# Prompt attention that keeps the weights of all query blocks by key block, and multiplies them with the values in products of up to 512 columns

## The chip, the cores and the metric

The kernel runs on one core of one Trainium2 chip. The metric is the device time of one execution in microseconds (us). An execution is also taken by the hardware profiler; its records are the trace from which all rows below come. The engines are called PE (TensorE, matrix products; PEld is its weight load), DVE (VectorE), ACT (ScalarE), POOL (GpSimd) and SP (SyncE, which here issues transfers). ACT and POOL issue transfers too.

## The reference

One inference step of a decoder with two layers and a width of 1024, for a prompt of 512 tokens and for 8 sequences of 4 new tokens each that have 2048 cached positions. Each layer normalises its input and runs three mixers on it: a stick-breaking attention (called sb here, 4 heads of 64), a forgetting attention (fox, 4 heads of 64) and a state-space scan. Gates merge the three, an output projection and a squared-ReLU MLP follow. Of the prompt the two attentions compute, cut to what matters:

```
def stick_breaking_core(q, k, v, q_pos, k_pos):
    z = einsum('bqhd,bkhd->bhqk', q, k) * (HEAD_DIM ** -0.5)
    mask = k_pos[None, :] < q_pos[:, None]
    log_keep = where(mask, log_sigmoid(-z), 0.0)
    later = cumsum(log_keep, axis=3, reverse=True) - log_keep
    w = where(mask, exp(log_sigmoid(z) + later), 0.0)
    return einsum('bhqk,bkhd->bqhd', w, v)

def forgetting_core(q, k, v, fq, fk, q_pos, k_pos):
    s = einsum('bqhd,bkhd->bhqk', q, k) * (HEAD_DIM ** -0.5) + (fq - fk)
    p = softmax(where(k_pos[None, :] <= q_pos[:, None], s, NEG_INF))
    return einsum('bhqk,bkhd->bqhd', p, v)
```

Both run over query blocks of 128 tokens. Query block b needs the key blocks 0 to b only.

## The kernel before

All tokens, 544 of them, stand in two halves of 272 columns (TH). Each weight matrix comes from memory in slabs `wr` and is split into a high part `wh` (by ACT) and a low part `wl` (by DVE); the activations are split in the same manner. A projection unit is then 24 products of 128 x 272: 16 with `wh` and 8 with `wl`, into the accumulators "g" or "z". Products of split operands pass PE once; products of plain fp32 operands, as all of those of the attention, pass it four times, and the trace keeps two records for each.

`prompt_attention` (L511) runs for sb and for fox in both layers. A pair c of heads stands in one tile of 128 rows, head e of the pair in rows 64e to 64e+63. For each c (2 of them) and each query block b (0 to 3) it multiplies queries with keys (L518: a row group of 64, n = 128(b+1) columns, one bank "z" for each head, rows `z<-half`), computes the weights on DVE, ACT and POOL (L521, tiles "tr"), turns each block of 128 x 128 of them on PE (L526, rows `t<-C,tr`), copies the turned blocks to the core's memory (ACT, L528) and multiplies them with the values (L533, 128 rows, 64 columns of PE for each head, rows `o<-tr,vn`): for key blocks k = 0 to b one product of 128 columns for either head. The result goes to y (ACT, L535). So there are 32 passes (c, b) in the program: 160 products with values and 64 with keys.

`weave` (L246) puts the generators of several parts of the program beside each other, so that PE has projection units between the steps of the attention. The scheduler of the tile framework, which knows what depends on what, then sets the final order on each engine; every engine runs its own list in order.

The cached keys and values are gathered by POOL's queue (L338, rows `kv<-in_cache_...`), 512 KB a piece. `Cached` (L565) issues gathers ahead, up to 7, into tiles of a pool `kvp` with 9 buffers; `take` hands them to the products. A buffer is free for the next gather when its last product has read it.

At the start ACT's queue gets the second half of x (L292, L293) right behind the parameters. While x comes, PE multiplies a tile of zeros with itself (L437). Then come the squares of x (ACT, L443), which a product with ones sums (`t<-ts,C`), and from these the first norm. `parameters` (L314) loads the page table and computes the indices `idx` of all gathers.

Of the kernel before, what the change touches and what calls it, by code (L numbers as in the profile page):

```python
# [174 lines left out]
def _trunk(ctx, tc, i, o, cc):  # L175
# [6 lines left out]
    hp = ctx.enter_context(tc.tile_pool(name="hp", bufs=11))  # L182
    kvp = ctx.enter_context(tc.tile_pool(name="kvp", bufs=9))
    tr = ctx.enter_context(tc.tile_pool(name="tr", bufs=4))
# [33 lines left out]
    def trt():  # L218
        return tr.tile([P, 512], F32, tag="tr", name="tr")

# [16 lines left out]
    def mm(out, w, x, **kw):  # L237
        n = float(np.prod(x.shape[1:]))
        pe["t"] += n * (1 if x.dtype == F32R else 4) * out.shape[0] / P / 2400
        nc.tensor.matmul(out, w, x, **kw)  # L240
# [50 lines left out]
    nc.scalar.dma_start(PC, i["params"])  # L291
    for u in range(2):  # L292
        nc.scalar.dma_start(x.tiles[u][:, :, TH:], i["x"][1, u])  # L293
    nc.gpsimd.dma_start(C[:, :P], i["consts"][:, :P])
# [137 lines left out]

    h = Feat(dtype=F32R), Feat(dtype=F32R)
    idle = trt()
    dve.memset(idle, 0.0)
    warm = bank("a")
    for _ in range(5):  # L437
        mm(warm, idle[:, :P], idle)
    for s in range(2):
        acc = bank("t")[:, :TH]  # L440
        for k in range(KD):
            q = tst()[:, :TH]
            act.activation(q, x.at(k, s * TH, (s + 1) * TH), AF.Square)  # L443
            mm(acc, ones, q, start=k == 0, stop=k == KD - 1)
        scaled(h, x, "norm1_g", 0, rsqrt(acc, 1.0 / D), s)
# [64 lines left out]

    def prompt_attention(r, y, weights):  # L511
        for c in range(2):
            for b in range(4):
                n = (b + 1) * P
                ws, wts, zs = [], [], [bank("z") for _ in range(2)]
                for e in (1, 0):
                    hr = slice(64 * e, 64 * e + 64)
                    mm(zs[e][:, :n], r["q"][hr, c, b * P:(b + 1) * P], r["kT"][hr, c, :n])  # L518
                for e in range(2):
                    ws.append(trt())  # L520
                    weights(ws[e], zs[e], n, 2 * c + e, b)  # L521
                yield 12.0
                for e in range(2):
                    pt = bank("t")
                    for k in range(b + 1):
                        turned(pt[:, k * P:(k + 1) * P], ws[e][:, k * P:(k + 1) * P], ident)  # L526
                    wts.append(trt())
                    act.copy(wts[e][:, :n], pt[:, :n])  # L528
                    yield 1.5
                acc = bank("o")[:, :P]  # L530
                for k in range(b + 1):
                    for e in range(2):
                        mm(acc[64 * e:64 * e + 64, :], r["vn"][:, k, (2 * c + e) * 64:(2 * c + e) * 64 + 64],  # L533
                           wts[e][:, k * P:(k + 1) * P], start=k == 0, stop=k == b)
                act.copy(y[:, c, b * P:(b + 1) * P], acc)  # L535
        r["prompt"] = True
# [120 lines left out]
    def sb_sample(l, r, y):  # L657
        k, v = "cache_sb_k", "cache_sb_v"
        jobs = key_jobs(l, k, 3)
        for c in (2, 1, 0):  # L660
            jobs += key_jobs(l, k, c) + value_jobs(l, v, c + 1)
        rows = Cached(jobs + value_jobs(l, v, 0), 7)
        rows.ahead()
# [37 lines left out]
    def fx_sample(l, r, y, sq):  # L701
# [3 lines left out]
        for c in (1, 2, 3):  # L705
            jobs += key_jobs(l, k, c) + value_jobs(l, v, c - 1)
        rows = Cached(jobs + value_jobs(l, v, 3), 7)
        rows.ahead()
# [520 lines left out]
    for l in range(DEPTH):  # L1229
# [8 lines left out]
        if l:  # L1238
            turn["tags"] = ("g",)
        run(some(gsb, 4))  # L1240
        if not l:
            parameters()
        run(some(gsb, 4))
        cs = conv_state(l)
# [121 lines left out]
```

## Time and profile before

| | us |
|---|---|
| Median of 3 runs (2012.42, 2017.52, 2018.73) | 2017.52 |
| Profiled execution | 2016.9 |
| Its span, from first to last instruction | 2014.9 |
| PE busy | 1946.5 (97%) |
| DVE busy | 1043.7 (52%) |
| ACT busy | 993.0 (49%) |
| POOL busy | 361.5 (18%) |
| Mean granted clock of PE | 0.988 |

The span is what the trace covers; the device time has 2.0 us more around it. A granted clock of 1 is 2.4 GHz, 0.5 is 1.2 GHz. A busy share is a mean over the span.

### The profile page before, as it was taken

How to read it: one execution, taken by the hardware profiler on the slowest of the kernel's cores; microseconds unless marked ns; L12 is line 12 of the kernel's file. 1: busy time of each engine (PE TensorE's matmuls, PEld its weight loads, DVE VectorE, ACT ScalarE, POOL GpSimd, SP SyncE). 2: the span in 40 equal slices, each digit the busy share in tenths (PEclk: the TensorE clock that was granted, in tenths of full speed). 3: DMA queues.
4: the chain of work that ended last, by engine and by line, in shares of the span. 5: the costliest groups of instructions: out<-in, count | busy, mean ns of one | idle time of the engine just before them, and what ended most of it. 6: DMA issues, size and time to landing. Idle time of an engine off the chain costs nothing.

```text
span 2014.9 us, 40892 instructions
## 1 busy us (share of the span) xinstructions
PE 1946.5 (97%) x17046; PEld 1803.4 (90%) x17046; DVE 1043.7 (52%) x2027; ACT 993.0 (49%) x2139; POOL 361.5 (18%) x430
## 2 busy tenths in 40 slices
PE   8999999999999999999999999999999999999997
PEld 7888777878899999999998887787788999999997
DVE  4475567545466444444555646684545554443445
ACT  5475557245565333333445645672566443333334
POOL 2233522243100000000023344213430000000000
PEclk9999999999999999999999999999999999999999
DMA  6665555487442233223356656537873412323222
GB/s 227 197 225 181 194 178 191 139 280 279 140 140 84 76 93 95 84 86 94 116 205 219 205 187 214 200 114 245 274 253 105 148 54 86 93 85 91 88 84 87
DMA packets 105932, 308.94 MB, mean 153 GB/s; under 512 B 17060, under 2 KB 33188, under 8 KB 105236
## 3 DMA queue, kind: packets, MB, share of 16 engines
q1 hardware_dynamic: 66740, 169.12, 27.2%
q0 software_dynamic: 37088, 134.86, 19.5%
q8 instruction: 133, 2.18, 0.4%
q10 hardware_dynamic: 1920, 2.37, 0.3%
q14 instruction: 51, 0.42, 0.1%
HBM read 291.74 MB, written 14.57 MB: 152 GB/s over the span
## 4 chain that ended last, share of the span: by engine, by line
PE 85%; DVE 4%; DMA 4%; ACT 4%; issue 2%; another core or an unknown queue 1%; POOL 1%; SPq 0%; DVEq 0%; ACTq 0%; POOLq 0%
PE g L240 51%; PE z L240 23%; PE s L240 4%; PE a L240 3%; PE o L240 2%; PE t L244 1%; DMA kv<-in_cache_sb_v_dram,idx 1%; DMA wr<-in_w_in_dram 1%; DMA kv<-rowsd 1%; DMA kv<-in_cache_fox_v_dram,idx 1%; DVE gt L423 1%; ACT wh L355 0%; DVE half L346 0%; DVE wl L356 0%
## 5 line engine op out<-in xcount | busy, mean ns | idle before, releaser
L240 PE MATMUL g<-half,wh 128*128 128x272 f32 x5504 | 813.4, 294 | 15.5 <-ACT gt L887 6.2
L240 PEld LDWEIGHTS g<-half,wh 128*128 128x128 f32 x5504 | 733.5, 191 | 56.0 <-issue 27.5
L355 ACT CAST wh<-wr 128x1024 fp32r<-128x1024 f32 x238 | 249.7, 1049 | 407.8 <-PE g L240 347.7
L240 PE MATMUL g<-half,wl 128*128 128x272 f32 x2752 | 427.8, 290 | 2.0 <-issue 1.9
L356 DVE TENSOR_TENSOR wl<-wr,wh 128x1024 fp32r<-128x1024 f32 x238 | 291.7, 1226 | 224.6 <-ACT wh L355 197.4
L240 PEld LDWEIGHTS g<-half,wl 128*128 128x128 f32 x2752 | 376.8, 190 | 6.5 <-issue 6.1
L240 PE MATMUL z<-half,wh 128*128 128x272 f32 x2112 | 309.4, 289 | 3.5 <-ACT half L345 3.5
L240 PEld LDWEIGHTS z<-half,wh 128*128 128x128 f32 x2112 | 282.9, 189 | 4.6 <-ACT half L345 4.0
L346 DVE TENSOR_TENSOR half<-gt,half 128x272 fp32r<-128x272 f32 x224 | 95.7, 438 | 154.0 <-ACT half L345 150.0
L240 PE MATMUL z<-half,wl 128*128 128x272 f32 x1056 | 165.6, 287 | 0.0
L338 POOL DMA_INDIRECT kv<-in_cache_sb_k_dram,idx x64 | 63.9, 998 | 565.5 <-PE g L240 493.1
L240 PEld LDWEIGHTS z<-half,wl 128*128 128x128 f32 x1056 | 145.4, 189 | 0.2
L1197 DVE TENSOR_TENSOR half<-half,g 128x272 f32<-128x272 f32 x128 | 56.0, 437 | 112.4 <-PE g L240 112.1
L345 ACT CAST half<-gt 128x272 fp32r<-128x272 f32 x224 | 93.0, 419 | 28.1 <-DVE gt L423 17.0
L240 PE MATMUL s<-kv,Q 128*32 128x128 f32 x2048 | 87.0, 283 | 10.7 <-issue 10.3
L1327 POOL TENSOR_TENSOR half<-half,gt 128x272 f32<-128x272 f32 x4 | 3.7, 946 | 495.2 <-ACT gt L401 495.2
L240 PEld LDWEIGHTS s<-kv,Q 128*32 128x32 f32 x2048 | 58.3, 112 | 33.5 <-issue 28.9
L1197 DVE TENSOR_TENSOR half<-half,z 128x272 f32<-128x272 f32 x128 | 55.6, 434 | 57.1 <-PE z L240 56.7
L338 POOL DMA_INDIRECT kv<-in_cache_sb_v_dram,idx x64 | 66.4, 1037 | 99.5 <-PE s L240 30.6
L240 PE MATMUL a<-kv,ts 128*32 128x256 f32 x1024 | 73.7, 396 | 8.8 <-DMA kv<-in_cache_sb_v_dram,idx 5.0
L338 POOL DMA_INDIRECT kv<-in_cache_fox_k_dram,idx x64 | 65.3, 1020 | 93.9 <-PE a L240 20.4
L338 POOL DMA_INDIRECT kv<-in_cache_fox_v_dram,idx x64 | 62.0, 968 | 101.0 <-PE s L240 51.5
(254 smaller groups left out, 2105.1 us busy)
## 6 DMA issues: line engine op xcount, KB each, us to landing
wr<-in_w_in_dram SPq DMA_DIRECT2D x98, 512.0 KB
wr<-in_w_up_dram SPq DMA_DIRECT2D x64, 512.0 KB
wr<-in_w_down_dram SPq DMA_DIRECT2D x64, 512.0 KB
wr<-in_w_o_dram SPq DMA_DIRECT2D x16, 512.0 KB
kv<-rowsd SPq DMA_DIRECT2D x12, 512.0 KB
kv<-in_state_ssm_dram SPq DMA_DIRECT2D x8, 512.0 KB
out_dram<-kv SPq DMA_DIRECT2D x8, 512.0 KB
wr<-in_w_ssm_out_dram SPq DMA_DIRECT2D x8, 512.0 KB
```

Of the source, the lines that this page charges most:

```text
L240: nc.tensor.matmul(out, w, x, **kw)
L244: nc.tensor.transpose(out, x, one)
L338: nc.gpsimd.indirect_dma_start(dst, None, rows, bass.IndirectOffsetOnAxis(ap=index, axis=0))
L345: act.copy(hi, src)
L346: dve.tensor_tensor(lo, src, hi.bitcast(F32), op=OP.subtract)
L355: act.copy(hi, raw)
L356: dve.tensor_tensor(lo, raw, hi.bitcast(F32), op=OP.subtract)
L423: dve.scalar_tensor_tensor(u, x.at(k, t0, t1), pc(gname, l, k), rb, op0=OP.mult, op1=OP.mult)
L1197: dve.tensor_tensor(x.at(m, t0, t1), x.at(m, t0, t1), b, op=OP.add)
L1327: pool.tensor_tensor(ot[:, k], ot[:, k], rb, op=OP.mult)
```

## The change

1. The turned weights of all four query blocks of a pair are kept in one tile "pt", ordered by key block: key block k holds the query blocks k to 3 side by side. When all four are there, one product for each head and key block, of (4 - k) x 128 columns, replaces those of 128 columns. One copy of 128 x 512 takes the result to y.
2. The two loads of the second half of x are issued by ACT behind the fourth square.
3. The warm-up is 16 products of 512 columns and 4 of 272 in single passes, instead of 5 of 512 in four passes.
4. To make room: the pool of the gathered pieces has 8 buffers instead of 9, the depth of `Cached` is 6 instead of 7, the pool "tr" has 3 buffers instead of 4, and the memory for descriptors of POOL's transfers is 8192 instead of 16384.
5. In layer 0 `parameters` runs one step of `qkv` earlier.

```
-    kvp = ctx.enter_context(tc.tile_pool(name="kvp", bufs=9))
+    kvp = ctx.enter_context(tc.tile_pool(name="kvp", bufs=8))
...
-        return tr.tile([P, 512], F32, tag="tr", name="tr")
+        return tr.tile([P, 512], F32, tag="tr", name="tr", bufs=3)
...
-    for u in range(2):
-        nc.scalar.dma_start(x.tiles[u][:, :, TH:], i["x"][1, u])
...
-    idle = trt()
-    dve.memset(idle, 0.0)
+    idle = tr.tile([P, 512], F32R, tag="tr", name="idle", bufs=3)
+    dve.memset(idle.bitcast(F32), 0.0)
     warm = bank("a")
-    for _ in range(5):
-        mm(warm, idle[:, :P], idle)
+    for n in 16 * (512,) + 4 * (TH,):
+        mm(warm[:, :n], idle[:, :P], idle[:, :n])
...
-            act.activation(q, x.at(k, s * TH, (s + 1) * TH), AF.Square)
+            square = act.activation(q, x.at(k, s * TH, (s + 1) * TH), AF.Square)
+            if s == 0 and k == 3:
+                with tc.issue_after(square.ins):
+                    for u in range(2):
+                        nc.scalar.dma_start(x.tiles[u][:, :, TH:], i["x"][1, u])
...
         for c in range(2):
+            wt = tr.tile([P, 2, 13 * P], F32, tag="pt", name="pt", bufs=1)
             for b in range(4):
...
                 for e in range(2):
-                    pt = bank("t")
+                    t = bank("t")
                     for k in range(b + 1):
-                        turned(pt[:, k * P:(k + 1) * P], ws[e][:, k * P:(k + 1) * P], ident)
-                    wts.append(trt())
-                    act.copy(wts[e][:, :n], pt[:, :n])
+                        turned(t[:, k * P:(k + 1) * P], ws[e][:, k * P:(k + 1) * P], ident)
+                    to = wt[:, e, b * P:b * P + (3 * b + 1) * P].rearrange("p (k t) -> p k t", t=P)[:, ::3]
+                    act.copy(to, t[:, :n].rearrange("p (k t) -> p k t", t=P))
                     yield 1.5
-                acc = bank("o")[:, :P]
-                for k in range(b + 1):
-                    for e in range(2):
-                        mm(acc[64 * e:64 * e + 64, :], r["vn"][:, k, (2 * c + e) * 64:(2 * c + e) * 64 + 64],
-                           wts[e][:, k * P:(k + 1) * P], start=k == 0, stop=k == b)
-                act.copy(y[:, c, b * P:(b + 1) * P], acc)
+            acc = bank("o")
+            for k in range(4):
+                for e in (1, 0):
+                    mm(acc[64 * e:64 * e + 64, k * P:], r["vn"][:, k, (2 * c + e) * 64:(2 * c + e) * 64 + 64],
+                       wt[:, e, 4 * k * P:(3 * k + 4) * P], start=k == 0, stop=k == 3)
+            act.copy(y[:, c, :NP], acc)
...
-        rows = Cached(jobs + value_jobs(l, v, 0), 7)
+        rows = Cached(jobs + value_jobs(l, v, 0), 6)
...
-        run(some(gsb, 4))
+        run(some(gsb, 3))
         if not l:
             parameters()
+        run(some(gsb, 1))
...
-    nc = _bacc.Bacc("TRN2", target_bir_lowering=False, num_devices=1)
+    nc = _bacc.Bacc("TRN2", target_bir_lowering=False, num_devices=1, dynamic_dma_scratch_size=8192)
```

The scheduler sets the order, so the change shows best in the lists of the engines. On PE, in layer 1 at the fox heads' pair c = 1, query block b = 3, this stood before (`s<-kv,Q` are products with cached keys, `t<-C,tr` turns of prompt weights, `o<-tr,vn` their products with values, `g` a projection unit):

```order
L240 MATMUL s<-kv,Q 32x128 x4
L244 MATMUL t<-C,tr 128x128 x4
L240 MATMUL o<-tr,vn 64x128
L240 MATMUL g<-half,wh 128x272 x16
L240 MATMUL g<-half,wl 128x272 x8
L240 MATMUL g<-half,wh 128x272 x4
L240 MATMUL g<-half,wl 128x272 x2
L240 MATMUL o<-tr,vn 64x128 x7
L244 MATMUL s<-C,ts 128x128 x4
```

The same place in the changed kernel:

```order
L240 MATMUL s<-kv,Q 32x128 x4
L244 MATMUL t<-C,tr 128x128 x4
L240 MATMUL g<-half,wh 128x272 x16
L240 MATMUL g<-half,wl 128x272 x8
L240 MATMUL g<-half,wh 128x272 x4
L240 MATMUL g<-half,wl 128x272 x2
L240 MATMUL o<-pt,vn 64x512 x2
L240 MATMUL o<-pt,vn 64x384 x2
L240 MATMUL o<-pt,vn 64x256 x2
L240 MATMUL o<-pt,vn 64x128 x2
L244 MATMUL s<-C,ts 128x128 x4
```

The single product with values ahead of the projection unit is gone, and the seven behind it, for this block, have become eight for all four blocks.

On PE, in layer 1 at the fox heads' pair c = 0, query block b = 3, its products with keys stood so before (`z<-half 128x512`, one for each head):

```order
L240 MATMUL o<-tr,vn 64x128
L240 MATMUL g<-half,wh 128x272 x8
L240 MATMUL g<-half,wl 128x272 x4
L240 MATMUL o<-tr,vn 64x128 x2
L240 MATMUL z<-half 128x512 x2
L244 MATMUL t<-C,tr 128x128 x3
L240 MATMUL g<-half,wh 128x272 x8
```

And so in the changed kernel:

```order
L240 MATMUL g<-half,wl 128x272 x8
L244 MATMUL t<-C,tr 128x128 x2
L240 MATMUL z<-half 128x512
L244 MATMUL t<-C,tr 128x128 x2
L240 MATMUL z<-half 128x512
L240 MATMUL g<-gt,C 128x272
L240 MATMUL g<-half,wh 128x272 x16
```

The two heads' products, which stood next to each other, have two turns of 128 x 128 between them. Over the whole program 11 of the 32 pairs of products with keys are parted before (2432 columns in all) and 18 after (5632 columns).

ACT's list at the start of the program, before (`ts<-half` are the squares of x, `wh<-wr` the high parts of the first weights):

```order
L291 DMA PC<-in_params_dram 128x140
L293 DMA half<-in_x_dram 128x4x272 x2
L443 ACTIVATE ts<-half 128x272 x4
L330 ACTIVATE mulc<-PC 64x1 x2
L355 CAST wh<-wr 128x1024
L443 ACTIVATE ts<-half 128x272 x2
L355 CAST wh<-wr 128x1024
L443 ACTIVATE ts<-half 128x272 x5
```

And in the changed kernel, whose lines have other numbers:

```order
L291 DMA PC<-in_params_dram 128x140
L441 ACTIVATE ts<-half 128x272 x4
L445 DMA half<-in_x_dram 128x4x272 x2
L328 ACTIVATE mulc<-PC 64x1 x2
L353 CAST wh<-wr 128x1024 x2
L441 ACTIVATE ts<-half 128x272 x7
L398 ACTIVATE gt<-t,epsb 128x272
```

The loads of the second half of x have moved behind four squares, and both casts stand ahead of the fifth square.

## Rows read from the trace of the kernel before

**Rows 1.** The profile's page: its first line, and busy time by engine.

```profile
span 2014.9 us, 40892 instructions
...
PE 1946.5 (97%) x17046; PEld 1803.4 (90%) x17046; DVE 1043.7 (52%) x2027; ACT 993.0 (49%) x2139; POOL 361.5 (18%) x430
```

**Rows 2.** Busy time by engine in two stretches, then granted clock, transfer share, GB/s.

```profile
250.00:400.00 150.00, 140.18 (x1231) 116.84 (x1232) 96.55 (x218) 80.59 (x208) 35.49 (x47) 0.96 0.51 166
550.00:1000.00 450.00, 449.75 (x3588) 448.92 (x3587) 213.89 (x372) 194.74 (x364) 0.00 (x0) 1.00 0.31 95
```

**Rows 3.** Groups of instructions by form, PE: busy us, mean ns, idle before.

```profile
L240 PE MATMUL o<-tr,vn 128*64 128x128 f32 x320 | 36.1, 286 | 0.0
```

**Rows 4.** The timeline of PE from 1482 us: start, duration, instruction, count of records.

```profile
1482.70 0.43 PE L240 MATMUL o<-tr,vn 128*64 128x128 f32 x2
1483.06 2.28 PE L240 MATMUL g<-half,wh 128*128 128x272 f32 x16
1485.17 1.15 PE L240 MATMUL g<-half,wl 128*128 128x272 f32 x8
1486.16 0.67 PE L240 MATMUL g<-half,wh 128*128 128x272 f32 x4
1486.66 0.41 PE L240 MATMUL g<-half,wl 128*128 128x272 f32 x2
1487.01 1.09 PE L240 MATMUL o<-tr,vn 128*64 128x128 f32 x14
1488.03 0.75 PE L244 MATMUL s<-C,ts 128*128 128x128 f32 x4
```

**Rows 5.** The timeline of PE from 305 us, brackets: idle before and releaser.

```profile
305.94 1.13 PE L240 MATMUL z<-half 64*128 64x512 f32 x4
307.00 0.87 PE L240 MATMUL o<-tr,vn 128*64 128x128 f32 x10
309.47 1.97 PE L240 MATMUL a<-kv,ts 128*32 128x256 f32 x32 [1.60 <-DMA kv<-in_cache_sb_v_dram,idx]
```

**Rows 6.** The timeline of PE from 284 us.

```profile
284.15 0.91 PE L240 MATMUL z<-half 64*128 64x384 f32 x2
284.99 0.52 PE L240 MATMUL g<-half,wh 128*128 128x272 f32 x2
```

**Rows 7.** Groups of instructions by form, ACT: the copies to y.

```profile
L535 ACT COPY half<-o 128x128 f32<-128x128 f32 x32 | 8.5, 265 | 5.1 <-PE o L240 4.5
```

**Rows 8.** The timeline of ACT from 5 us.

```profile
5.21 1.39 ACT L443 ACTIVATE ts<-half 128x272 f32<-128x272 f32 x4 [3.11 <-DMA half<-in_x_dram]
...
10.96 1.04 ACT L355 CAST wh<-wr 128x1024 fp32r<-128x1024 f32 x1 [4.18 <-DMA wr<-in_w_in_dram]
...
16.33 0.49 ACT L400 ACTIVATE gt<-t,epsb 128x272 f32<-128x272 f32 x1 [0.48 <-PE t L240]
```

**Rows 9.** The timeline of PE from 8 us.

```profile
8.15 2.00 PE L240 MATMUL t<-ts,C 128*128 128x272 f32 x8
12.38 3.91 PE L240 MATMUL t<-ts,C 128*128 128x272 f32 x8 [2.24 <-ACT ts L443]
```

**Rows 10.** Busy time by engine from 14 to 16 us, then granted clock.

```profile
14.00:16.00 2.00, 2.00 (x5) 1.18 (x4) 1.11 (x3) 1.45 (x5) 0.00 (x0) 0.50 0.79 225
```

**Rows 11.** Transfer queues from 2 to 9.3 us: packets, MB, time share.

```profile
q1 hardware_dynamic: 1255, 1.87, 74.9%
q10 hardware_dynamic: 667, 0.57, 24.8%
```

**Rows 12.** Waits of PE, whole span: what for, us, times, longest.

```profile
PE a L240 <- DMA kv<-in_cache_sb_v_dram,idx: 5.0, 4, 2.1
...
PE a L240 <- ACT gt L638: 2.2, 1, 2.2
```

**Rows 13.** Waits of POOL, whole span.

```profile
POOL kv L338 <- PE s L240: 139.7, 37, 20.1
```

**Rows 14.** Tile kv, 290 to 312 us: ns min/median/max, first and last start.

```profile
L338 POOL DMA_INDIRECT kv<-in_cache_sb_v_dram,idx x2: 939/1028/1117, 299.6 to 300.9; - x2
```

More of the change, by code (lines that the diff above doesn't have):

```diff
@@ L512, in prompt_attention @@
         for c in range(2):
+            wt = tr.tile([P, 2, 13 * P], F32, tag="pt", name="pt", bufs=1)
             for b in range(4):
                 n = (b + 1) * P
-                ws, wts, zs = [], [], [bank("z") for _ in range(2)]
+                ws, zs = [], [bank("z") for _ in range(2)]
                 for e in (1, 0):
@@ L706, in fx_sample @@
             jobs += key_jobs(l, k, c) + value_jobs(l, v, c - 1)
-        rows = Cached(jobs + value_jobs(l, v, 3), 7)
+        rows = Cached(jobs + value_jobs(l, v, 3), 6)
         rows.ahead()
```

## The prediction

> **What bounds the kernel now.** I read the busy times first. PE is busy for 97% of a span of 2014.9 us, no other engine for more than 52% [rows 1]. The windows then show where the rest lies: from 550 to 1000 us PE is busy for 449.75 of 450 us at full clock, while in a stretch with prompt attention, 250 to 400 us, it is busy for 140.2 of 150 at a granted clock of 0.96 [rows 2]. So in most places a product that PE no longer does, or does faster, comes off the end, as long as its next work is ready. The sum below is therefore one of PE's list, place by place, and what DVE, ACT and POOL save counts for nothing unless PE waits for them. It is made against the profiled execution's 2016.9 us, which is 0.03% below the median of the three runs, 2017.52.
>
> Two prices are needed. **A change of form:** PE's products come in forms (128 rows x 128 columns for projections, 64 x 128 for keys, 128 x 64 for prompt values, 128 x 32 for cached rows). Eight `wl` products stand from 1485.17 to 1486.16, 0.124 us each; the two at 1486.66 are followed by products with values at 1487.01, 0.35 us later instead of 0.25 [rows 4]. So a change of form costs about 0.10 us. The Trainium skill, page TensorEngine Tiling (Array Packing), section Key Properties, says that changing the mode of tiling drains TensorE; this trace agrees, with that 0.10 us.
>
> **A column:** two products with keys of 512 columns, one for each head, take from 305.94 to 307.00, 1.06 us [rows 5]; one alone of 384 columns takes from 284.15 to 284.99, 0.84 [rows 6]. That the pair takes only 0.22 more says that the heads of a pair run beside each other, and 0.22 us for 128 columns is 1.7 ns a column. With 1.67, 512 columns are 0.85 and 384 are 0.64, and both rows leave 0.20 for the form's entry and exit.
>
> **The products with values.** The 320 records before are busy for 36.1 us [rows 3]. In PE's timeline they stand in 60 stretches, because the scheduler puts the first product ahead of the other head's copy. By records: 35 stretches of 2, from start to next start 0.36 us (1482.70 to 1483.06) [rows 4]; 2 of 4 (0.37), 3 of 6 (0.58), 4 of 8 (0.59), 7 of 10 (0.80), 2 of 12 (0.81) and 7 of 14 (1.02, from 1487.01 to 1488.03) [rows 4]. These sum to 31.9 us; with 60 entries of 0.10 they hold PE for 37.9. (The 1.02 of fourteen records, which are seven products of 0.21 us, also says that heads run beside each other in this form.) After, a group has 512 + 384 + 256 + 128 = 1280 columns a head: 1280 x 1.67 ns = 2.13 us and 0.20 for entry and exit, 2.33. Eight groups are 18.7; the order shows one, layer 0's fox pair c = 0, cut into three pieces, which costs two entries and exits and some columns without a partner, 0.8. So 19.5 for 37.9: **-18.4 us.**
>
> **What the new order gives back.** The scheduler now parts 18 pairs of products with keys where it parted 11, with 5632 columns in place of 2432. Parted heads no longer run beside each other: 3200 x 1.67 ns = 5.3 us, and seven more entries and exits, 1.4: **+6.7.** Counted over PE's whole order there are 465 changes of form before and 403 after, 62 fewer. The values take 100 away (60 stretches to 10, two each), the parted pairs add 14, so 24 others came: turns and cached rows that stood side by side with value products now stand between projections. 24 x 0.10: **+2.4.** Sum of PE's stream: -9.3.
>
> **Copies.** ACT's 32 copies to y take 8.5 us [rows 7]; 8 of 512 columns replace them. PE never stood idle ahead of a value product (the 0.0 at the end) [rows 3], so what feeds them is early enough, and ACT, busy for 49% [rows 1], is not behind: 0.
>
> **The start.** The fifth square can't be made before a cast that stands ahead of it in ACT's list; that cast waits until 10.96 for the first weights [rows 8]. PE sums four squares until about 10, then waits 2.24 us until 12.38, and needs 3.91 us for the other four [rows 9], since its clock there is 0.50, the lower level [rows 10], after that wait. The norm follows at 16.33 [rows 8]. In the changed order both casts stand ahead of that square, 2.1 us instead of 1.04, but the weights come sooner: up to about 6.6 us (the end of the fourth square) ACT's queue carries nothing large, and in the trace it held 24.8% of the engines' time from 2 to 9.3 us beside SP's 74.9% [rows 11]. About 6 us of a quarter are 1.5 us; so the casts go from about 9.5 to 11.6 and the squares from 11.9 in a row. With PE at half clock (0.98 a product) the norm is at about 16.0, with full clock at 14.3. I take -0.7, near the half clock that the row has; bounds 0 and -2.0. The warm-up ends near 7.7 instead of 8.15 and hides: PE waits for squares behind it anyway; without that cover it would be 0.4 us.
>
> A rule speaks against this gain. The Trainium skill, page DMA: Bandwidth & Descriptors, section Queues, rings and completion order, says that a DMA engine takes turns between the queues that have work, a packet each. By it the deferred loads would, once issued, have half of the turns, and what the weights gained until 6.6 us would be lost again: the start's term is then 0 and the sum 2008.6. The row speaks of 3 to 1 in time for the whole window, but with larger transfers on SP's queue, and decides nothing between them.
>
> **Fewer buffers for gathers.** A gather can start when its buffer has been read: POOL waited 139.7 us in 37 waits for products with cached keys [rows 13], so one buffer fewer does start gathers later. What counts is PE's work between a buffer's last reader and the first reader of what comes into it. From the order with the trace's durations: its median over 96 takes falls from 19.1 to 17.8 us, those under 8 us go from 13 to 15, the least from 6.4 to 5.1. The last gather for the product at 309.47 was issued at 300.9 [rows 5, 14], so where transfers are dense 8.6 us lie between issue and use, and 8 us of cover are about where waits begin. Before, PE waits for gathered sb values in 4 takes, 5.0 us in all [rows 12]; the worst, 1.60 at 309.47 [rows 5] and its like in layer 1, get wider (7.4 to 11.6 us, 7.4 to 10.5), while others get tighter. I take +1.0; bounds -4 and +17 (0.18 us in each take). The earlier `parameters` and the smaller descriptor memory: 0: the first lets gathers begin one unit of 24 products sooner (3.1 us, from 1483.06 to 1486.16) [rows 4] and not later; POOL needs about 1 us for one gather's descriptors [rows 14] and waits for buffers, not for descriptors [rows 13]; without that cover it would be some 1 us in each late take.
>
> 2016.9 - 9.3 - 0.7 + 1.0 = 2007.9, so **2008.0 us**, own range 2002 to 2011.5. Its ends: below, the 24 new changes of form cost nothing (-2.4), the start gives -2.0 instead of -0.7 and the gathers -1.0 instead of +1.0, 5.7 in all; above, each of the 24 costs 0.2 (+2.4) and the gathers twice what I take (+1.0).
>
> **Rivals.** *Waits go too (13%).* The 1.60 and 2.1 us waits for sb values vanish with the wider places, and so does the 2.2 us wait for a small copy [rows 12], since in the new order 24 products of projections stand ahead of it. A wait of that size can bring a spell at half clock behind it: the 3.91 us behind the 2.24 us wait [rows 9, 10] are 2.0 more than at full clock; two such spells less are 4.0. 2016.9 - 9.3 - 0.7 - 3.7 - 2.2 - 4.0 = 1997.0. Against it: the waiting place may only move.
>
> *Given back as waits (24%).* Values of a pair now wait for the last of four query blocks, with a single "pt" tile: the copies of the next pair's first block must wait for the group. Where this leaves PE without work it waits about 1.9 us, like those that stand in the table of waits [rows 12], and pays a half-clock spell, 2.0. Two of these: 2006.9 + 7.8 = 2014.7, not to be told from no change.
>
> *Slower (8%): the gathers become the bound.* With depth 6, if the wait in each of 96 takes grows by over 0.17 us, the sum passes 2023. At 0.18 it is 2006.9 + 17 = 2024. For it: places of 5.1 us against the 8.6 us above. Against: only 15 takes lie under 8 us, and 13 did before with 5.0 us of waits. Wide values that don't run beside each other would give the same, 8 x 2.13 = 17 us; the 1.02 us above speaks against that.
>
> **Chances.** 0.3% (6 us) is about what a measurement of this kernel can tell from no change: faster is below 2011.5, slower above 2023.6. The forecast has 55%, all of its own range below 2011.5; with the 13% faster is 68%, same 24%, slower 8%. The range that leaves out the slower case and half of the best one is 1998 to 2015.
>
> **What would show it.** In the trace after: 8 groups `o<-pt,vn` of about 2.3 us each and near 19 us in sum; parted `z<-half` products of 512 columns taking 0.85 + 0.2 us each; squares five to eight in a row from about 11.9 us and the norm at 14.3 to 16.0; waits for `kv` under 8 us in sum. Wrong is the sum if value groups take over 3 us, if waits of PE for `kv` or for ACT's copies into "pt" exceed 8 us, or if the granted clock falls below 0.98.

## The result, and the profile after

The changed kernel takes 1994.94 us (median of 4 runs, 1992.4 to 1995.43) where the kernel before takes 2015.12 beside it (4 runs): a ratio of 0.989, 95% interval 0.9866 to 0.9913, so 18 to 27 us faster. The prediction was 2008.0 with a range of 1998 to 2015: the sign was right, the gain more than twice what was forecast. The profiled execution took 1994.71 us, 22.2 less than that of before.

The page of the changed kernel begins so:

```profile
span 1993.0 us, 40474 instructions
...
PE 1927.8 (97%) x16864; PEld 1791.6 (90%) x16864; DVE 1037.8 (52%) x2027; ACT 996.2 (50%) x2115; POOL 370.5 (19%) x430
```

PE is busy for 18.7 us less than in [rows 1] and still bounds the kernel. The two windows of [rows 2], after:

```profile
250.00:400.00 150.00, 141.25 (x1300) 118.04 (x1301) 93.25 (x215) 83.74 (x209) 41.38 (x49) 0.98 0.56 189
550.00:1000.00 450.00, 449.75 (x3587) 448.85 (x3586) 213.67 (x374) 191.11 (x356) 4.59 (x5) 1.00 0.31 96
```

From 250 to 400 us PE passes 1300 records where it passed 1231, though not quite the same work stands in the same window; from 550 to 1000 us nothing moved. The groups of PE by form that answer to [rows 3]:

```profile
L240 PE MATMUL o<-pt,vn 128*64 128x512 f32 x32 | 8.6, 618 | 0.0
L240 PE MATMUL o<-pt,vn 128*64 128x384 f32 x32 | 6.5, 486 | 0.0
L240 PE MATMUL o<-pt,vn 128*64 128x256 f32 x32 | 5.5, 381 | 0.0
L240 PE MATMUL o<-pt,vn 128*64 128x128 f32 x32 | 3.2, 276 | 0.0
```

The same place as in [rows 4], in PE's timeline after:

```profile
1463.09 0.41 PE L240 MATMUL g<-half,wl 128*128 128x272 f32 x2
1463.43 2.37 PE L240 MATMUL o<-pt,vn 128*64 128x512 f32 x16
1465.73 0.75 PE L244 MATMUL s<-C,ts 128*128 128x128 f32 x4
```

A group of all four key blocks holds PE for 2.30 us, from 1463.43 to 1465.73 (2.33 was the estimate with its entry). Two parted products with keys of 512 columns, in the timeline after (the pair of [rows 5] took 1.06 us together):

```profile
302.87 1.12 PE L240 MATMUL z<-half 64*128 64x512 f32 x2
303.92 1.14 PE L240 MATMUL g<-half,wl 128*128 128x272 f32 x7
...
305.24 1.12 PE L240 MATMUL z<-half 64*128 64x512 f32 x2
306.29 2.00 PE L240 MATMUL g<-half,wh 128*128 128x272 f32 x14
...
312.22 1.96 PE L240 MATMUL a<-kv,ts 128*32 128x256 f32 x32
```

Each takes 1.05 us alone, as priced. The last line is the products with cached values that waited 1.60 us in [rows 5]: there is no wait now (why is taken up below). The start, on ACT and then on PE, beside [rows 8, 9]:

```profile
8.60 1.04 ACT L353 CAST wh<-wr 128x1024 fp32r<-128x1024 f32 x1 [1.41 <-DMA wr<-in_w_in_dram]
9.90 1.04 ACT L353 CAST wh<-wr 128x1024 fp32r<-128x1024 f32 x1 [0.26 <-DMA wr<-in_w_in_dram]
10.86 1.39 ACT L441 ACTIVATE ts<-half 128x272 f32<-128x272 f32 x4
...
15.16 0.49 ACT L398 ACTIVATE gt<-t,epsb 128x272 f32<-128x272 f32 x1 [0.42 <-PE t L240]
```

```profile
7.31 1.99 PE L240 MATMUL t<-ts,C 128*128 128x272 f32 x8
11.34 3.79 PE L240 MATMUL t<-ts,C 128*128 128x272 f32 x8 [2.04 <-ACT ts L441]
```

The first weights come at 8.60 instead of 10.96, the squares stand in a row from 10.86, and PE, after a wait of 2.04 us, needs 3.79 us for products that take about 2 at full clock; the norm comes at 15.16 instead of 16.33. The waits of PE, to be read beside [rows 12]:

```profile
PE g L240 <- ACT gt L892: 10.2, 2, 6.3
PE s L240 <- issue: 8.8, 21, 1.0
PE z L244 <- DVE tr L497: 7.7, 4, 2.9
PE s L240 <- DMA kv<-in_cache_fox_k_dram,idx: 6.9, 5, 3.2
PE g L240 <- issue: 4.2, 8, 0.8
```

The figures are the sum in us, the number of waits and the longest. "issue" stands for waits of which the trace names no cause. Both waits of [rows 12] are gone, and others have grown: for the gate's copy on ACT (`gt`; 6.2 before), for fox keys (none before), and for a bank that the sb weights hold (1.7 before). And the place of the 2.2 us wait:

```profile
385.19 0.27 PE L244 MATMUL s<-C,zn 128*32 128x128 f32 x1
385.21 2.25 PE L240 MATMUL g<-half,wh 128*128 128x272 f32 x16
387.31 1.17 PE L240 MATMUL g<-half,wl 128*128 128x272 f32 x8
388.31 0.41 PE L240 MATMUL g<-half,wh 128*128 128x272 f32 x2
388.65 1.09 PE L240 MATMUL a<-vn,gt 32*32 32x512 f32 x8
389.67 2.48 PE L240 MATMUL s<-kv,Q 128*32 128x128 f32 x81
```

Between the turn of the new tokens' weights and their products stand 26 products of projections, and PE goes on without a wait.

### The profile page after: what moved, and what is told of

Same layout as the page of the kernel before. It is cut to its first block, busy times and chain, and to the rows that moved or that the text cites. A ratio compares the mean times of both kernels' runs of the same rounds, so it can differ in the third digit from the quotient of the medians.

```text
span 1993.0 us, 40474 instructions
## 1 busy us (share of the span) xinstructions
PE 1927.8 (97%) x16864; PEld 1791.6 (90%) x16864; DVE 1037.8 (52%) x2027; ACT 996.2 (50%) x2115; POOL 370.5 (19%) x430
## 4 chain that ended last, share of the span: by engine, by line
PE 87%; DVE 3%; DMA 3%; issue 2%; ACT 2%; POOL 1%; SPq 0%; another core or an unknown queue 0%; DVEq 0%; POOLq 0%; ACTq 0%
PE g L240 52%; PE z L240 24%; PE s L240 4%; PE a L240 3%; PE o L240 2%; PE t L244 1%; DMA kv<-in_cache_fox_k_dram,idx 1%; DMA raw<-rowsd 1%; DVE gt L421 1%; DMA wr<-in_w_in_dram 1%; DMA kv<-rowsd 0%; PE t L240 0%; PE s L244 0%; DVE half L344 0%; DMA wr<-in_w_down_dram 0%
## 5 line engine op out<-in xcount | busy, mean ns | idle before, releaser
L240 PE MATMUL g<-half,wh 128*128 128x272 f32 x5504 | 809.8, 293 | 16.5 <-ACT gt L892 10.2
L240 PE MATMUL s<-kv,Q 128*32 128x128 f32 x2048 | 80.1, 277 | 15.9 <-issue 8.8
L336 POOL DMA_INDIRECT kv<-in_cache_sb_v_dram,idx x64 | 72.5, 1133 | 103.3 <-PE a L240 27.6
L892 ACT COPY gt<-g 128x272 f32<-128x272 f32 x112 | 42.4, 380 | 76.8 <-PE g L240 62.4
```

Source lines behind the costliest of these rows:

```text
L336: nc.gpsimd.indirect_dma_start(dst, None, rows, bass.IndirectOffsetOnAxis(ap=index, axis=0))
L892: act.copy(c, unit(w, 0, h, s))
```

## The experiments

The same two programs gave two levels of time. Before took 2013 to 2015 us in the first comparison and in three of the series below, and 1973 to 1974 in the two others, so each run is compared with before in its own series. The record gives chip number 1 for the first series (2014 us) and for the second (1973 us), so the level does not seem to be a property of a chip. Each run has its ratio to before with the 95% interval.

| run | what is in it | median, before beside it (us) | ratio, interval |
|---|---|---|---|
| e1_start | start only | 2003.98, 2014.28 | 0.9951 (0.9936 to 0.9967) |
| e2_values | wide products and their room | 1991.65, 2014.28 | 0.9897 (0.9873 to 0.9921) |
| e3_heads | heads 1, 0; 128 columns | 2019.45, 2014.28 | 1.0027 (1.0007 to 1.0046) |
| e4_no_values | all but the wide products | 2023.65, 2014.28 | 1.0065 (1.0039 to 1.0092) |
| e5_room | buffers only | 1984.48, 1973.41 | 1.0053 (1.0035 to 1.0071) |
| e6_after | full change | 1968.02, 1973.41 | 0.9976 (0.9966 to 0.9985) |
| e7_q_dve | full change, zeros by DVE | 1968.65, 1973.41 | 0.9977 (0.9963 to 0.9991) |
| e8_warm | warm-up only | 1977.59, 1973.41 | 1.0021 (1.0012 to 1.003) |
| e9_before | before again | 2013.5, 2012.97 | 1.0009 (0.9993 to 1.0025) |
| e10_after | full change | 1992.32, 2012.97 | 0.9905 (0.9887 to 0.9923) |
| e11_values | as e2_values | 1994.16, 2012.97 | 0.9905 (0.9886 to 0.9924) |
| e12_start | as e1_start | 2003.79, 2012.97 | 0.9952 (0.9938 to 0.9966) |
| e13_wide01 | full change, heads 0, 1 | 2001.4, 2014.17 | 0.9938 (0.9916 to 0.9961) |
| e14_heads_start | heads 1, 0 and start | 2012.68, 2014.17 | 1.0003 (0.9981 to 1.0026) |
| e15_wn_dve | one copy by DVE | 2018.27, 2014.17 | 1.0028 (1.001 to 1.0046) |
| e16_heads_start_wn | e14 with that copy | 2014.31, 2014.17 | 1.0001 (0.9983 to 1.0019) |
| e17_heads_start_deep | e14, 10 buffers | 1976.32, 1973.69 | 1.001 (0.9998 to 1.0023) |
| e18_before_deep | before, 10 buffers | 1989.65, 1973.69 | 1.0076 (1.0061 to 1.0091) |

To see where time went, PE's span is split in one way for every trace: from each product's start to the next one's start, idle time of over 0.2 us put apart, and the rest counted at full clock, so that what half clock adds is a row of its own. The clock's record begins 3 to 6 us after PE's first product; the warm-up until then is in the row "all the rest". The row of keys holds 4.3 to 4.7 us of other small products `z<-half`. The traces are of single runs: that of e3_heads took 2010.03 us, 9 below its median, and that of e8_warm 1972.23, 5 below. In us:

```
                       before  e9_before   after  e10_after  e3_heads  e14_heads_start  e12_start   e8_warm  e6_after
products with values     32.4       32.1    19.2       19.2      24.0             24.0       32.5      32.3      19.2
products with keys       34.8       34.9    41.8       41.8      41.0             41.7       34.0      35.0      41.6
projections            1594.3     1594.3  1589.0     1589.5    1591.1           1589.0     1593.2    1591.0    1586.8
turns of weights         20.0       20.6    18.3       18.5      17.8             17.6       19.9      19.8      18.0
cached scores            79.3       78.0    75.9       75.6      79.4             78.5       75.7      68.1      66.2
idle over 0.2 us         56.3       57.6    54.0       50.3      56.1             61.0       52.0      37.9      41.3
added by half clock      21.0       14.7    20.0       16.9      24.6             25.4       17.1      10.4      16.2
all the rest            166.4      167.3   164.2      164.7     163.3            163.9     165.2     165.3     164.5
sum                    2004.5     1999.5  1982.4     1976.5    1997.3           2001.1     1989.6    1959.8    1953.8
```

**Parts alone (first series).** e1_start has the later loads and the warm-up; e2_values has the new `prompt_attention` and the smaller buffers; e3_heads changes one line of before; e4_no_values is the full change with the old `prompt_attention` and four "tr" buffers.

```
# e3_heads
                 for k in range(b + 1):
-                    for e in range(2):
+                    for e in (1, 0):
                         mm(acc[64 * e:64 * e + 64, :], ...
```

> Only the start is changed (loads of the second half of x behind the fourth square, warm-up in single passes); everything else is as before. Theory 1 (the start gives what the landmarks of the two traces show, the first weights in use at 18.4 instead of 19.6 us and the third slab at 40.2 instead of 43.2): 3 us faster, about 2012. Theory 2 (the start gives only what its own arithmetic shows, the rest of these 3 us came with the attention's order): 0.7 to 1.3 us faster, not to be told from no change.

> The wide products with values and the smaller buffers that make room for them (gathered pieces 8 and depth 6, three tr tiles, half the descriptor memory); start and place of the page table's load as before. Theory 1 (what PE's list saves, priced form by form, is all: 465 to 404 changes of form, value products 29.0 to 18.1 us, parted products with keys 29.4 to 36.9, in sum 5 us by list): 2008 to 2011. Theory 2 (the wide products also take away waits and half-clock spells of PE, some 9 us, which is what the prediction missed): 1996 to 2000. If 2, its trace has fewer waits or less half-clock work than before at the same places as the full change.

> The kernel before with one change: the products with values take the heads of a pair in the order 1, 0 instead of 0, 1. The products keep 128 columns and one copy for each query block. Theory 1 (the gain lies in the stretches, not in the columns: with this order the scheduler no longer puts a single product ahead, 422 changes of form instead of 465): by PE's list 5.9 us faster, 2009. Theory 2 (the wide columns are needed): within 2 us of before. Theory 3 (any new order of the attention shifts waits by as much as PE's list changes): anything from 2003 to 2017, and its waits, not its list, say why.

> Everything but the wide products: start, depth 6 and 8 buffers, half the descriptor memory, earlier page table; values as before, four tr tiles. Theory 1 (fewer buffers cost, +1 us, the start gives 3): 2013. Theory 2 (fewer buffers cost nothing, or shift gathers to better times): 2005 to 2012. A rival from the prediction (gathers become late): 2020 or more, with waits of PE for kv above 10 us.

The wide products with their smaller buffers give all of the gain (22.6 us), and the start alone gives 10 us, half of it: the parts do not add. Both are more than either of their theories allowed. The heads' order alone makes the products with values and keys 2 us shorter in sum, projections 3 and turns 2 to 3, and yet its median is 5 us above before, outside all three theories. Its trace, of a faster run, is no longer than those of before, so it does not show those 5 us. In its waits stands

```profile
PE a L240 <- DMA kv<-in_cache_sb_v_dram,idx: 10.1, 4, 3.6
```

where before had 5.0 [rows 12], and half clock added 24.6 us (21.0 and 14.7 before). Without the wide products the smaller buffers cost: e4_no_values is 20 us slower than e1_start, as the rival had it, and PE waited there for fox keys,

```profile
PE s L240 <- DMA kv<-in_cache_fox_k_dram,idx: 15.0, 8, 3.3
```

**Room, the full change again, one wait, the warm-up (second series).** e5_room has kvp 8, depth 6 and half the descriptor memory only; e8_warm the new warm-up only. e7_q_dve adds to the full change:

```
-        pool.memset(Q, 0.0)
+        dve.memset(Q, 0.0)
```

> The kernel before with the smaller buffers only: 8 for gathered pieces, depth 6, half the descriptor memory. By PE's list it costs 1.8 us (products with keys parted as after the full change). Theory 1 (fewer buffers make gathers late and PE's waits throw it to half clock): 2023 or more, 9 us or more over before, with waits for gathered rows above 10 us and over 25 us lost at half clock. Theory 2 (the loss of the run without the wide products came from its own order, not from the buffers): 2012 to 2018.

> The full change again, to compare it with the wide products alone on one chip. Theory 1 (the start adds its own 1.2 us to the wide products): 1 to 3 us faster than they were, 1989 to 1991. Theory 2 (start and wide products each move waits and half-clock spells, and these do not add): 1992 to 1997, so no faster than the wide products alone (0.9897 of before).

> The full change, with one more edit: the block of zeros of the cached queries is written by DVE instead of POOL, where it stands in line behind gathers that wait for buffers; ACT waited 2.06 us for it, and behind ACT PE waited 2.9 us for a bank, once in each layer. Theory 1 (that wait is real on PE's path): 5.8 us of waits gone, 1988 to 1990. Theory 2 (what PE waits for there is late in another way too, or the wait moves on): 1993 to 1996.

> The kernel before with the single-pass warm-up only, which ends ahead of the data that PE waits for, and otherwise moves a few products of the first unit. Theory 1 (what stands in PE's list and waits is all that counts): within 1 us of before. Theory 2 (a small shift at the start changes which later stretches run at half clock): more than 3 us either way, with waits and list as before and another sum of half-clock time.

Here the full change gives 5.4 us, not 20. Buffers alone cost 11 us, as theory 1 had it; the wait for fox keys is 9.0 us, that for sb values is gone. Half clock, which theory 1 put above 25 us, adds 15.5. In e7_q_dve the wait that was aimed at went and another grew; its waits and, above them, those of e6_after:

```profile
PE g L240 <- ACT gt L892: 9.8, 2, 6.1
PE z L244 <- DVE tr L497: 7.7, 4, 2.9
PE s L240 <- DMA kv<-in_cache_fox_k_dram,idx: 7.0, 7, 2.3
```

```profile
PE g L240 <- ACT gt L892: 14.0, 2, 7.9
PE s L240 <- DMA kv<-in_cache_fox_k_dram,idx: 7.9, 6, 4.0
...
PE z L244 <- DVE tr L497: 1.9, 2, 0.9
```

5.8 us off one and 4.2 onto the other: the time did not move. The warm-up alone is 4 us slower; a few products of the first unit change places with it, so the cause is not settled.

**Before, the full change and its parts side by side (third series).** No new edits.

> The kernel before, unchanged, for a profile and a time on the same chip as the next three. The first two series ran at 2014 and 1973 us for the same program, and PE's waits of which the trace names no cause (issue) were 18.3 us in the first trace and none in those of the second series. Theory 1 (these waits are the chip's or the session's, not the kernel's): if the time is near 1973, no such waits and 8 to 16 us less than before in waits of under 0.2 us; if near 2014, some 18 us of them again. Theory 2 (they are the program's): some 18 us whatever the time.

> The full change on the same chip. Theory 1 (the gain has a part that PE's list carries, some 10 us, and a part that hangs on how starved PE is of instructions, 5 to 10 us): 4 to 10 us faster than before where the waits without a cause are near 0, 18 to 22 where they are near 18. Theory 2 (half-clock time by chance decides): anything between, with the sum lost at half clock as the difference.

> The wide products with their room alone on the same chip. Theory 1 (as the full change without the start): within 3 us of it, 4 to 10 us faster than before on a chip with few waits without a cause. Theory 2 (wide products gave all of the 22.6 us because of something that stays): 20 us or more faster on any chip.

> The start's edits alone on the same chip. Theory 1 (the start gives what its landmarks show, and what came behind them in the first series were other waits and half-clock time): 2 to 5 us faster. Theory 2 (the 10 us of the first series are its own): 8 to 12 us faster on any chip.

At 2013 us the waits with no cause in the trace are back. e9_before first, then e10_after:

```profile
PE s L240 <- issue: 10.0, 24, 1.0
PE g L240 <- issue: 6.1, 13, 1.1
```

```profile
PE s L240 <- issue: 9.2, 23, 1.2
...
PE g L240 <- issue: 4.6, 9, 0.8
```

In the second series e6_after, the same program, has no such wait. Over all traces these waits sum to 11.5 to 18.9 us in each of the 14 at the slower level and to 0.2 us or less in each of the 6 at the faster one. So they belong to the series and not to the program. The full change gains 20.6 us and the start 9.2 here, as in the first comparison and the first series: theory 1 of e12_start (2 to 5) fell. The wide products alone gain 18.8, so the start adds nothing to them that can be told apart.

**Width or order, and the wait in layer 0 (fourth series).** e13_wide01 writes `for e in range(2)` over the wide products; e14_heads_start joins e3_heads and e1_start; e15_wn_dve and e16_heads_start_wn change in before and in e14_heads_start:

```
-        act.copy(wn, b[:NS, :P])
+        dve.tensor_copy(wn, b[:NS, :P])
```

> The full change with one difference: the wide products with values take the heads in the order 0, 1, as the kernel before did. By PE's list there are 426 changes of form instead of 403, and heads of a pair do not run beside each other where the first is put ahead. Theory 1 (what shortens PE's list is that nothing stands between the heads of a pair, not the width): about 10 us slower than the full change, within 10 us of before. Theory 2 (the width does it): within 3 us of the full change.

> The kernel before with the order of heads 1, 0 and the start's edits: products of 128 columns, all buffers as before. Theory 1 (list and waits both count: the heads' order took 10 us off the list but left the waits and half-clock time of layer 0, which the start's edits took away): 15 to 20 us faster where before takes 2014, as fast as the full change. Theory 2 (the wide products are needed): no faster than the start alone, 0.995 of before.

> The kernel before with one copy (the turned weights of the new tokens, for which PE waits 2.2 us once in layer 0, ahead of two half-clock stretches) made by DVE instead of ACT. Its list of PE is 4.6 us longer. Theory 1 (that wait starts the half-clock stretches of layer 0, and both go): 3 to 8 us faster in spite of the list. Theory 2 (the half-clock stretches come from elsewhere): 0 to 5 us slower.

> The heads' order, the start's edits and the copy by DVE together, as a candidate against the full change. Theory 1 (the wait for that copy is gone already with the start's edits): as the second run within 3 us. Theory 2 (it was still there in part): 3 to 6 us faster than the second run.

With the heads in the order 0, 1 the wide products lose about a third of the gain (0.9938 for 0.9905 in the third series; the intervals just meet), which is between the two theories. With the order 1, 0 and 128 columns nothing is gained at all, though its values, keys, projections and turns are in sum within 4 us of the full change's. Idle time is 61.0 us and half clock adds 25.4 (52.0 and 17.1 in e12_start), and the wait for sb values is

```profile
PE a L240 <- DMA kv<-in_cache_sb_v_dram,idx: 10.1, 3, 5.0
```

The copy by DVE did not take its wait away: PE waited 3.5 us in two places for it, and the kernel was slower. Theory 1 fell in e14_heads_start and e15_wn_dve; in e16_heads_start_wn it held, since that run is within 2 us of e14_heads_start.

**One more buffer (fifth series).** kvp 10, depth 8, half the descriptor memory, in e14_heads_start and in before.

> The heads' order and the start's edits with 128-column products, now with one buffer more for gathered pieces (10, depth 8; half the descriptor memory makes room). Without the buffer PE waited 10.1 us for sb values. Theory 1 (what the shorter list saves is lost at gathers that come late): the waits for sb values fall below 4 us and it is 5 to 10 us faster than before. Theory 2 (these waits have another cause than a missing buffer): they stay at 8 us or more and the time at that of before.

> The kernel before with the same extra buffer, as the control. PE's list is 4 us longer by its order. Theory 1 (one buffer fewer cost 0.53%, so one more gives something): waits for gathered rows go, and it is 0 to 5 us faster. Theory 2 (at 9 buffers the gathers wait for PE's order, not for room): 2 to 6 us slower, by its longer list.

The waits for sb values did not fall. e17_heads_start_deep and e18_before_deep:

```profile
PE a L240 <- DMA kv<-in_cache_sb_v_dram,idx: 11.0, 2, 6.4
```

```profile
PE a L240 <- DMA kv<-in_cache_sb_v_dram,idx: 7.1, 2, 3.7
```

All eleven traces with 9 or 10 buffers have this wait (3.6 to 12.8 us), and of the nine with 8 buffers only one (1.0); these have waits for fox keys of 3.2 to 15.0 instead, which the others have at 4.0 or less. So the number of buffers, with the depth that goes with it, decides which of the gathers comes late, not whether one does.

## Why the prediction was right in sign and wrong in size

Against the mean of the two traces of before, the mean of the two after is 22.6 us shorter (2002.0 to 1979.4); the sum had said 9.0. The split says where: values -13.0, keys +7.0, projections -5.0, turns -1.9, cached scores -2.9, idle -4.8, half clock +0.6, the rest -2.4.

**Products with values (-18.4 with their entries): right.** From their first start to what follows they lost 13.0 us, where 31.9 less 18.5 (ten stretches without their entries) had been 13.4; the rest of the term was entries, which the split books with other products.

**Parted products with keys (+6.7): right.** The products of 64 rows alone grew by 6.6 us; 5.3 for the columns and 0.7 for seven exits had been 6.0.

**Other changes of form (+2.4): wrong.** What is booked with projections and turns, the entries saved and those that were to come back, should have been about -1.9 (62 fewer changes less the 50 exits of value stretches, plus 7 of keys: 19 at 0.10). It was -6.9; in the second series, between e8_warm and e6_after, -6.0. Even if the 24 changes that came back cost nothing, only -4.3 is explained (43 at 0.10); what saved the rest is open. This is some 5 us of the miss.

**The start (-0.7): the norm's mechanism right, the size low.** Squares in a row from 10.86 (predicted 11.9), the norm 1.2 us sooner and at half clock in this trace; in e1_start PE waited 1.22 instead of 2.04 us there, stayed at full clock, and the norm came at 13.67:

```profile
11.53 2.10 PE L240 MATMUL t<-ts,C 128*128 128x272 f32 x8 [1.22 <-ACT ts L441]
```

That is 2.7 us sooner, somewhat beyond the lower bound of -2.0 (a norm at 14.3). But the edit alone gave 10.3 and 9.2 us (e1_start, e12_start), far outside the bounds of 0 and -2.0: the term followed the norm only and took all that comes behind it as fixed. The weights came 2.4 us sooner, where 1.5 was the estimate. The transfer queues from 2 to 9.3 us, after, to be read beside [rows 11]:

```profile
q1 hardware_dynamic: 1470, 2.28, 91.7%
q10 hardware_dynamic: 265, 0.13, 8.2%
```

ACT's queue moved 0.13 MB, which is what its constants and parameters come to (64 and 70 KB). The loads of x, issued at 5.50 and 6.16 us, had moved nothing by then: their first packet starts at 9.43, 3.9 us after the first issue (before, 3.8 us: issued at 1.75, first packet at 5.53). Once they move, both queues have work; from 10 to 11 us, after:

```profile
q10 hardware_dynamic: 269, 0.29, 93.6%
q1 hardware_dynamic: 264, 0.03, 21.4%
```

269 packets of one queue and 264 of the other agree with what the Trainium skill, page DMA: Bandwidth & Descriptors, section Queues, rings and completion order, says of turns between queues. The rival that drew on it failed on the time: the second weights were in use at 9.90, when the loads of x had only just begun to move.

**Fewer buffers (+1.0): too small for the edit alone, and not to be read off in the full change.** Alone, the buffers cost 11.1 us (e5_room), inside the bounds of -4 and +17. With the wide products the waits for gathered rows are 6.9 and 4.4 us in sum (after, e10_after), where they were 5.2 and 4.9 before.

**Waits without a cause and cached scores, put at nothing: this step failed, beside the changes of form.** The sum had one term for waits, +1.0 for late gathers. The table of PE's waits of before, from which [rows 12] are cut, begins with a line that it left out, and has a second two lines below:

```profile
PE s L240 <- issue: 10.3, 27, 1.0
...
PE g L240 <- issue: 6.0, 12, 0.8
```

No term stood for these, and no reason was given. PE's whole table of waits, in us (it counts waits from 0.15 us on):

```
                    before  e9_before   after  e10_after  e12_start   e8_warm  e6_after
no cause (issue)      18.3       18.6    13.7       14.5       18.5       0.2       0.0
with a named cause    40.1       40.7    42.3       38.4       35.6      40.0      43.0
```

Waits with a named cause are the same before and after (40.4 in the mean of two): what the prediction held against its rival, that the waiting place may only move, came true. Waits without a cause fell by 4.4 us, and the cached scores by 2.9 (by 1.9 in the second series), for which the sum had no term either. With the 5 us of changes of form that is 12 of the 13.6 us by which the sum missed; what is left lies in the row "all the rest". Why the full change has fewer waits without a cause is open. At the faster level, which has none, it gives 5.4 us, less than the 9.0 of the sum: there, between e8_warm and e6_after, values, keys, projections and turns lose 12.5 us, but named waits take back 3.0 and half clock 5.8.

**The rival at 1997.0 came within 2 us of the result by luck.** Its two waits, for sb values and for the small copy, did go in the full change. But both also went in e5_room, with the old products, which is 11 us slower than before: the wait for sb values is gone or 1.0 in every trace with 8 buffers, so the smaller pool is enough to remove it, without wider places. The wait for the small copy is absent from 16 of the 20 traces, among them e3_heads, e4_no_values, e14_heads_start and e18_before_deep, none of them faster than before. Other waits grew in their place (fox keys 6.9, the bank 7.7, the gate's copy 10.2), and of its 4.0 us at half clock nothing came (17.9 to 18.5). None of the signs that the prediction named as wrong appeared either: groups of 2.30 us, waits for `kv` of 6.9, for the copies into "pt" of 1.7, a clock of 0.987. They looked only for a result that is too slow.

Why the parts do not add is open too. The start alone and the wide products alone both lose the wait for the small copy, but so do slower kernels, so that wait is not what they share. In the split both shorten the cached scores (78.7 to 75.7 and 76.5 with the start, to 75.0 and 74.2 with the wide products), and the full change does so only once (75.9 and 75.6); beyond these 2 to 4 us nothing is shown.

**Open.** Why a list as short gives 20 us with wide products and nothing with 128 columns in the heads' order is only half answered: with 128 columns the gain was taken back as idle time and half clock, with sb values waiting 10 us. More buffers did not help; the heads' order with 8 buffers was not tried, nor the earlier page table by itself. The two levels of time, too, have no cause here. No run beat the full change: the wide products alone were as fast where both ran in one series.

## What to carry to other kernels

On an engine that is busy for 97%, sum the list of products place by place, but give waits a term of their own with both signs, those without a named cause too: here values, keys, projections and turns explained 13 of 23 us. A wait that goes is no proof that its going brought the gain: look whether it went in the slower runs too. An edit that shortens the list ahead of a late transfer may only lengthen the wait for it, so test a saving with and without the reordering that comes with it. Gains of two edits measured alone (20 and 10 us here) need not add, and a gain found on one level of time (20 us) can be a quarter of that on another.

## What the runs showed of the hardware

The same program ran at 2013 to 2015 us in some series and at 1973 in others, with nearly the same granted clock (0.987 and 0.989 for the full change). Product by product, most of the difference of 28.6 us between the two traces of the full change lies in dense runs of cached scores (75.9 and 66.2 us) and in idle time (54.0 and 41.3): in the slower series PE halts in places after four to six records (two for each product) for some 0.3 us with no cause in the trace. After, at 392 us, these lines are

```profile
392.32 0.44 PE L240 MATMUL s<-kv,Q 128*32 128x128 f32 x5 [0.17 <-issue]
393.05 0.44 PE L240 MATMUL s<-kv,Q 128*32 128x128 f32 x6 [0.29 <-issue]
393.79 0.42 PE L240 MATMUL s<-kv,Q 128*32 128x128 f32 x4 [0.30 <-issue]
```

and in e6_after the same products, 96 records from 380.58 us on, run without such a halt. Within a series the time follows the granted clock: 12 runs of e1_start go from 1998.45 us at 0.993 to 2006.42 at 0.988, and 24 of before from 2006.59 at 0.992 to 2019.25 at 0.986. So single runs of one program lie 8 and 13 us apart here, roughly in step with the granted clock; in e14_heads_start it is 21 us (2007.22 at 0.986 to 2028.18 at 0.976). At the start of the two kernels the loads that ACT issued began to move 3.8 and 3.9 us after their issue.
